# Adding the second direction's decay from PSUM on VectorE, with a third buffer for the decay rows

## The chip, the cores and the metric

The kernel runs on one core of one Trainium2 chip. The time is the device time of one execution in microseconds (us); of several runs the median is given. The engines are TensorE (PE in the profile, its weight loads PEld), VectorE (DVE), ScalarE (ACT), GpSimd (POOL) and SyncE (SP), which here only issues DMAs. The program is built by a tile framework: the code says what is computed and how many buffers each kind of tile has, and a scheduler puts the instructions of each engine in an order. Each engine then works through its own list strictly in that order.

## The reference

One inference step of a two-layer diffusion backbone over T = 1280 tokens (256 context, 1024 latent). Layer 0 is latent attention beside a convolution module; layer 1 is a bidirectional state-space mixer (SSD). The change lies in layer 1's scan, which the reference computes once per direction, in chunks of 128 tokens:

```
a_cum  = cumsum(dt * a_neg)                      # per chunk and head
decay  = exp(where(causal, a_cum[l] - a_cum[s], -inf))
cb     = einsum('bclgn,bcsgn->bclsg', c, b)
y_diag = einsum('bclsg,bclsge,bcsgep->bclgep', cb, decay, x * dt)
states = einsum('bcsgn,bcsge,bcsgep->bcgepn', b, exp(a_end - a_cum), x * dt)
prev   = scan over chunks: s = s * exp(a_end) + states
y_off  = einsum('bclgn,bcgepn,bclge->bclgep', c, prev, exp(a_cum))
y      = y_forward + flip(y_backward) + d_skip * x
out    = rmsnorm(y * silu(z)) @ w_out
```

The two directions share `x`, `b` and `c`; only the decays and the states differ.

## The kernel before

The kernel runs in stages: projection, convolution and attention of layer 0, the output projection and norm, then layer 1. Large matmuls are done as three products of split operands (`mm3`, lines 119 to 121).

The scan is a loop over eight passes `u` (four of the 32 heads each) and ten chunks `c` (lines 1219 to 1276). While pass `u` is scanned, the input projection and convolution of pass `u + 1` (`in_blocks`) and the gate blocks (`z_block`) are computed, and the backward states of pass `u + 1` are advanced, one chunk for each chunk scanned (`back_states`, through `bk`). Pass 7 has no next pass; its companions are the first parts of the output projection (`part_c`, tile `yh`, `yl`).

For a chunk, `scan_a` (line 1129) makes the 128x128 decay matrix of four heads for each direction: a matmul of the cumulated sums (`lt`, `mv`; line 1136) and one that adds the mask (line 1140) into a PSUM tile, and the exponential on ScalarE into an SBUF tile `et` (line 1141). GpSimd adds the two directions' tiles (line 1148), VectorE multiplies the sum by `cb` (line 1149). `scan_b` (line 1152) then takes the product of the states with `c` (line 1161) and of the decay with `x` (line 1166) into two more PSUM tiles, and VectorE puts them together: line 1170 multiplies by the rows `eb`, line 1175 sums over directions, 1178 and 1179 finish `y`. The squares of `y` are written into `eb` by ScalarE (1181) and added up by GpSimd (1183, 1184); only then is that `eb` free. `advance` (line 1070) steps a state: VectorE weights `x` (`xw`, line 1075), a matmul (1078), GpSimd scales the old state (1083), VectorE adds the matmul's result (1085). The backward `advance` first loads its own operand `bx` (line 1073).

PSUM has eight tiles here: three "mm" for the projections, one "tm" for transposes and four "sd", which the scan's tiles share in turn: two decay tiles, in even passes one for `cb`, the two of `scan_b`, and one for each `advance`.

Each chunk's inputs come by DMA: `xa` (three buffers), `eb` (two buffers, three DMAs, lines 1123 and 1126), `bx` (two), the mask rows `mv` and `lt` (two pairs of buffers, lines 1113 and 1114), `bt` and the prepared states `pl`. `y` goes out at line 1265, backward states at 1100. All stand in the one queue of SyncE, in order: a DMA whose buffer isn't free holds up all behind it.

The scheduler orders each engine's list by a simulated timeline, so an edit in one place moves instructions elsewhere as well.

Of the kernel before, what the change touches and what calls it, by code (L numbers as in the profile page):

```python
# [10 lines left out]
F32 = mybir.dt.float32  # L11
# [3 lines left out]
AF = mybir.ActivationFunctionType  # L15
# [41 lines left out]
def _body(nc, tc, d, es, dbg, stop):  # L57
    V, S, G, PE = nc.vector, nc.scalar, nc.gpsimd, nc.tensor
    dma = nc.sync.dma_start

    def pool(name, bufs=1, space=None, side=None, stack=es):
        kw = {}
        if space is not None:
            kw["space"] = space
        if side is not None:
            kw["side"] = side
        if space is None:
            kw["reuse_waits"] = "tile"
        return stack.enter_context(tc.tile_pool(name=name, bufs=bufs, **kw))
# [17 lines left out]
    def psum(tag="x"):  # L87
        tag = tag if tag in ptags else "sd"
        p, n = ptags[tag]
        return p.tile([128, 512], F32, name="ps" + tag, tag=tag, bufs=n)  # L90
# [91 lines left out]
    def bcast_cols(r, j0, jn, ps):  # L182
        for j in range(jn):
            PE.matmul(ps[:, j * 128:(j + 1) * 128], r[:, j0 + j:j0 + j + 1].to_broadcast([128, 128]), ident,
                      start=True, stop=True)
        return ps
# [246 lines left out]
    for c0, n in CHUNKS:  # L433
        ps = psum()
# [86 lines left out]
    for c0, n in CHUNKS:  # L521
        ps = bcast_cols(rq, c0 // 128, n // 128, ps=psum("pt"))
# [366 lines left out]
    def dtile(name, dt=F32, tag=None):  # L889
        return dq.tile([128, HT], dt, name=name, tag=tag or name)  # L890
# [40 lines left out]
    p = dtile("p")  # L931
# [43 lines left out]
    for half in range(2):  # L975
        hs = slice(half * 64, half * 64 + 64)
        for c0 in range(0, 5):
            c = half * 5 + c0
            ps = psum("sd")
# [77 lines left out]
    sp = pool("ssd", bufs=2, side="right", stack=esC)  # L1057
# [50 lines left out]
    xas, ebs, cbs, bts = {}, {}, {}, {}  # L1108
# [7 lines left out]
    def load_x(u, c):  # L1116
        xa = xas[c] = sp.tile([128, OXD], F32, name="xa", tag="xa", bufs=3)
        dma(xa, cmb[u, c, :, 0:OXD])
        if u % 2 == 0:
            bts[c] = sp.tile([128, 128], F32, name="bt", tag="bt")  # L1120
            dma(bts[c], cmb[u, c, :, OBT:OBT + 128])
        eb = ebs[c] = sp.tile([128, 2, 3, 128], F32, name="eb", tag="eb")
        dma(eb[:, :, 2], cmb[u, c, :, OXD:OXD + 256].rearrange("p (j t) -> p j t", j=2))
        for pr_ in range(2):
            ev = eyd[c, 4 * u:4 * u + 4].rearrange("(j p) d t -> p j (d t)", p=2)[pr_]
            dma(eb[pr_ * 64:pr_ * 64 + 64, :, 0:2].rearrange("p j d t -> p j (d t)"),
                ev.unsqueeze(0).to_broadcast([64, 2, 256]))

    def scan_a(u, c):
        xa = xas[c]  # L1130
        ct = xa[:, OCT:OCT + 128]
        mv, lt = mvs[c % NMV], lts[c % NMV]
        pss = [psum("sd") for _ in range(2)]
        es_ = [sp.tile([128, 4, 128], F32, name="et", tag="et", bufs=4) for _ in range(2)]
        for dr, ps in enumerate(pss):
            PE.matmul(ps, lt[:, dr], mv, start=True, stop=False)  # L1136
        for dr, ps in enumerate(pss):
            et = es_[dr].rearrange("p h t -> p (h t)")
            p3, mk = ps.rearrange("p (h t) -> p h t", h=4), maskb[:, dr:dr + 1].to_broadcast([128, 4, 128])
            PE.matmul(p3, identb, mk, start=False, stop=True)  # L1140
            S.activation(et, ps, AF.Exp)  # L1141
        if u % 2 == 0:
            pc_ = psum("sd")
            PE.matmul(pc_[:, :128], bts[c], ct, start=True, stop=True)
            cbs[c] = sp.tile([128, 128], F32, name="cb", tag="cb", bufs=NCH)
            S.copy(cbs[c], pc_[:, :128])
        mt = es_[0]
        G.tensor_add(mt, es_[0], es_[1])  # L1148
        V.tensor_mul(mt, mt, cbs[c].unsqueeze(1).to_broadcast([128, 4, 128]))
        return xa, mt  # L1150

# [67 lines left out]
    for u in range(8):  # L1219
# [9 lines left out]
        elif u:  # L1229
            z_block(2 * u)  # L1230
            z_block(2 * u + 1)
        load_x(u, 0)
        load_x(u, 1)
        if u == 7:
            esK.close()
# [4 lines left out]
            for k in range(14):  # L1240
                prep_y(0, k, None, yp[k < 6], "yhl")
        nxt = scan_a(u, 0)
        sf = None
        for c in range(NCH):
            cur, nxt = nxt, (scan_a(u, c + 1) if c + 1 < NCH else None)
            if c + 2 < NCH:
                load_m(u, c + 2)
# [11 lines left out]
            if c + 2 < NCH:  # L1259
                load_x(u, c + 2)  # L1260
# [281 lines left out]
```

## Time and profile before

| | us |
|---|---|
| median of 3 runs (2082.36 to 2091.7) | 2087.28 |
| the profiled execution, whole | 2085.1 |
| its span, first to last instruction | 2083.3 |
| TensorE busy | 1999.5 |
| VectorE busy | 1391.4 |
| ScalarE busy | 876.8 |
| GpSimd busy | 707.3 |

Busy time says how much of the span an engine had an instruction at work; TensorE's matmuls overlap, and the end of one is modelled, so that 96% doesn't mean full speed. The granted clock is the mean over the stretch of TensorE's two levels, 1.2 and 2.4 GHz, with 2.4 as 1. An idle time is put down to what ended it. The scan runs from about 1094 to 1880 us: the first chunk's mask matmul starts at 1094.4 us, and the last product of a decay tile at 1876.3 us.

### The profile page before, as it was taken

To read this page: it belongs to the slowest core of one execution; us is meant where nothing else is said; L and a number is where in the kernel's file an instruction comes from. 1 tells how busy PE (TensorE), PEld (TensorE's weight loads), DVE (VectorE), ACT (ScalarE), POOL (GpSimd) and SP (SyncE) were. 2 spreads that over 40 slices of the span, in tenths; PEclk is the share of its full clock that TensorE was granted. 3 is DMA by queue.
4 is the path that set the end of the run, shared out by engine and by line. 5 is a ranking of instruction groups with operands and counts; after the bars stand their busy time and mean duration, and the time that the engine had idled before them with its cause. 6 is when DMAs were issued, how large, how long until landed. Compare 5 with 4: busy or idle time off the path is not lost. (4 is left out here: it accounts for less than half of the span.)

```text
span 2083.3 us, 32430 instructions
## 1 busy us (share of the span) xinstructions
PE 1999.5 (96%) x11830; PEld 1629.6 (78%) x11830; DVE 1391.4 (67%) x2177; ACT 876.8 (42%) x1683; POOL 707.3 (34%) x567
## 2 busy tenths in 40 slices
PE   6999999999999999989999999999999999789997
PEld 4777888777777768868887878887788877579997
DVE  5797897666565763357658586758587666773743
ACT  5411311666565663234644343443344333334531
POOL 1211122213131212543125465545464444552101
PEclk9999999999999999999999999999999999999998
DMA  8424123220222225322567767765776577655442
GB/s 331 170 107 149 53 93 122 75 68 29 62 61 60 67 84 206 124 88 79 163 197 227 223 182 216 227 193 178 214 218 192 178 228 221 210 155 203 133 163 71
DMA packets 273341, 313.57 MB, mean 151 GB/s; under 512 B 21184, under 2 KB 221920, under 8 KB 273184
## 3 DMA queue, kind: packets, MB, share of 16 engines
q1 hardware_dynamic: 273184, 311.51, 47.6%
q8 instruction: 94, 1.54, 0.3%
q14 instruction: 63, 0.52, 0.1%
HBM read 223.38 MB, written 88.05 MB: 149 GB/s over the span
## 5 line engine op out<-in xcount | busy, mean ns | idle before, releaser
L119 PE MATMUL psmm<-hl,wh 128*128 128x512 f32 (+1 forms) x1152 | 424.1, 368 | 4.6 <-ACT wh L114 3.4
L121 PE MATMUL psmm<-hl,wl 128*128 128x512 f32 (+1 forms) x1152 | 422.2, 367 | 4.2 <-POOL wl L115 4.2
L120 PE MATMUL psmm<-hl,wh 128*128 128x512 f32 (+1 forms) x1152 | 423.7, 368 | 0.0
L115 POOL TENSOR_TENSOR wl<-ws,wh 128x1024 fp32r<-128x1024 f32 x89 | 224.5, 2524 | 464.2 <-ACT wh L114 462.1
L121 PEld LDWEIGHTS psmm<-hl,wl 128*128 128x128 f32 x1152 | 218.7, 190 | 36.9 <-POOL wl L115 6.2
L119 PEld LDWEIGHTS psmm<-hl,wh 128*128 128x128 f32 x1152 | 219.0, 190 | 35.9 <-ACT wh L114 4.3
L120 PEld LDWEIGHTS psmm<-hl,wh 128*128 128x128 f32 x1152 | 219.0, 190 | 30.1 <-issue 1.2
L383 DVE SCALAR_TENSOR_TENSOR cacc<-cvin,acw,cacc 128x1295 f32<-128x1295 f32 x120 | 206.9, 1741 | 4.6 <-ACT cacc L378 3.1
L114 ACT CAST wh<-ws 128x1024 fp32r<-128x1024 f32 x109 | 113.5, 1042 | 206.4 <-PE psmm L120 149.2
L848 DVE SCALAR_TENSOR_TENSOR cy<-raw,prm,cy 128x1282 f32<-128x1282 f32 x96 | 162.9, 1697 | 23.6 <-ACT cy L845 15.7
L120 PE MATMUL psmm<-hlo,wh 128*128 128x512 f32 (+3 forms) x480 | 171.4, 358 | 0.0
L119 PE MATMUL psmm<-hh,wh 128*128 128x512 f32 (+3 forms) x480 | 167.7, 359 | 1.7 <-ACT hh L259 1.7
L121 PE MATMUL psmm<-hh,wl 128*128 128x512 f32 (+3 forms) x480 | 169.2, 355 | 0.0
L617 DVE TENSOR_REDUCE mx<-pss 128x1 f32<-128x512 f32 (+1 forms) x208 | 137.3, 668 | 35.3 <-PE pss L121 34.3
L119 PE MATMUL psmm<-yh,wh 128*128 128x256 f32 (+1 forms) x476 | 148.2, 315 | 3.3 <-ACT yh L1205 2.8
L120 PE MATMUL psmm<-yl,wh 128*128 128x256 f32 (+1 forms) x476 | 150.0, 317 | 0.5 <-DVE yl L1206 0.3
L1148 POOL TENSOR_TENSOR et<-et 128x512 f32<-128x512 f32 x80 | 125.1, 1564 | 72.1 <-ACT et L1141 69.7
L121 PE MATMUL psmm<-yh,wl 128*128 128x256 f32 (+1 forms) x476 | 147.8, 314 | 1.4 <-POOL wl L115 1.4
L1083 POOL TENSOR_TENSOR st<-st,dec_bc 128x256 f32<-128x256 f32 x104 | 82.9, 803 | 168.6 <-DVE st L1085 113.4
L626 ACT ACTIVATE prob<-pss,nm 128x512 f32<-128x512 f32 x192 | 130.2, 693 | 16.1 <-DVE nm L621 14.2
L646 PE MATMUL pspt<-ident,prob 128*128 128x128 f32 x800 | 121.7, 278 | 4.7 <-ACT prob L626 3.8
L652 ACT COPY ptile<-pspt 128x512 f32<-128x512 f32 (+1 forms) x144 | 81.2, 568 | 105.3 <-PE pspt L646 104.3
(336 smaller groups left out, 4151.1 us busy)
## 6 DMA issues: line engine op xcount, KB each, us to landing
xa<-cmb SPq DMA_DIRECT2D x80, 384.0 KB
wm<-in_wmod_dram SPq DMA_DIRECT2D x48, 512.0 KB
ws<-in_wc_dram SPq DMA_DIRECT2D x40, 512.0 KB
eb<-eyd SPq DMA_DIRECT2D x160, 128.0 KB
ws<-in_wco_dram SPq DMA_DIRECT2D x32, 512.0 KB
cmb<-xt SPq DMA_DIRECT2D x24, 640.0 KB
bx<-cmb SPq DMA_DIRECT2D x72, 192.0 KB
eb<-cmb SPq DMA_DIRECT2D x80, 128.0 KB
```

Source lines behind the costliest of these rows:

```text
L114: S.copy(wh, ws)
L115: (eng or G).tensor_sub(wl, ws, f32(wh))
L119: PE.matmul(ps, lh, rh, start=start, stop=False)
L120: PE.matmul(ps, lh, rl, start=False, stop=False)
L121: PE.matmul(ps, ll, rh, start=False, stop=stop_)
L383: V.scalar_tensor_tensor(cacc[i], cv[:, k:k + CO], acw[:, 31 * i + k:31 * i + k + 1], cacc[i], ALU.mult, ALU.add)
L617: V.tensor_reduce(mx[:, x:x + 1], ps[:, :n], axis=AX.X, op=ALU.max, negate=len(segs) == 1)
L626: S.activation(prob[:, c:c + n], ps[:, :n], AF.Exp, bias=nm, accum_out=sums[:, x:x + 1])
L646: PE.transpose(ps[:, x * 128:(x + 1) * 128], prob[:, (g + x) * 128:(g + x + 1) * 128], ident)
L848: V.scalar_tensor_tensor(y, raw[:, k:k + RO], ccw[:, 5 * blk + k:5 * blk + k + 1], y, ALU.mult, ALU.add)
L1083: G.tensor_mul(n.rearrange("p (h e) -> p h e", e=64), s.rearrange("p (h e) -> p h e", e=64), dec_ap(u, dr, c))
L1148: G.tensor_add(mt, es_[0], es_[1])
```

## The change

Three edits in two functions. The second direction's exponential is written back into its own PSUM tile and not into an `et` tile. VectorE adds it from there to the first direction's tile, in place of GpSimd's addition of two SBUF tiles. So there is one `et` tile a chunk, and of these three buffers, where there were four buffers for two a chunk. The rows `eb` get three buffers and not two.

```diff
-        eb = ebs[c] = sp.tile([128, 2, 3, 128], F32, name="eb", tag="eb")
+        eb = ebs[c] = sp.tile([128, 2, 3, 128], F32, name="eb", tag="eb", bufs=3)
...
         pss = [psum("sd") for _ in range(2)]
-        es_ = [sp.tile([128, 4, 128], F32, name="et", tag="et", bufs=4) for _ in range(2)]
+        mt = sp.tile([128, 4, 128], F32, name="et", tag="et", bufs=3)
         for dr, ps in enumerate(pss):
             PE.matmul(ps, lt[:, dr], mv, start=True, stop=False)
         for dr, ps in enumerate(pss):
-            et = es_[dr].rearrange("p h t -> p (h t)")
             p3, mk = ps.rearrange("p (h t) -> p h t", h=4), maskb[:, dr:dr + 1].to_broadcast([128, 4, 128])
             PE.matmul(p3, identb, mk, start=False, stop=True)
-            S.activation(et, ps, AF.Exp)
+            S.activation(ps if dr else mt.rearrange("p h t -> p (h t)"), ps, AF.Exp)
...
-        mt = es_[0]
-        G.tensor_add(mt, es_[0], es_[1])
+        V.tensor_add(mt, mt, pss[1].rearrange("p (h t) -> p h t", h=4))
         V.tensor_mul(mt, mt, cbs[c].unsqueeze(1).to_broadcast([128, 4, 128]))
```

The new addition is line 1146 of the changed kernel and the multiplication line 1147; lines behind it are two lower than before.

Since the scheduler orders anew, the lists of all engines differ from the first chunk on. Three places matter. The first is SyncE's queue near the end of pass 6, before the change: `yz_16809` is the store of chunk 5, and `bx_16908` is the operand of the backward state step that goes with chunk 6.

```order
L1118 DMA xa_16834<-cmb_8593 128x768
L1106 DMA pl_16873<-pvd_9085 128x256
L1123 DMA eb_16772<-cmb_8593 128x2x128
L1126 DMA eb_16772<-eyd_8597 64x2x256 x2
L1100 DMA pvd_9085<-st_16848 128x256
L1121 DMA bt_16902<-cmb_8593 128x128
L1265 DMA yzd_8594<-yz_16809 128x2x128
L1118 DMA xa_16900<-cmb_8593 128x768
L1073 DMA bx_16908<-cmb_8593 128x384
```

The `bx` of chunk 6 stands behind the store of chunk 5; those of chunks 7 and 8 stand further on, between the stores of chunks 6 and 7. The same queue after the change: `yz_16742` is the store of chunk 5, and `bx_16905` the operand that goes with chunk 7.

```order
L1121 DMA bt_16834<-cmb_8593 128x128
L1114 DMA lt1_9078<-ltd_8596 8x128
L1123 DMA eb_16771<-cmb_8593 128x2x128
L1126 DMA eb_16771<-eyd_8597 64x2x256 x2
L1100 DMA pvd_9085<-st_16781 128x256
L1073 DMA bx_16905<-cmb_8593 128x384
L1113 DMA mv1_9077<-mvd_8595 2x512
L1263 DMA yzd_8594<-yz_16742 128x2x128
```

Now the `bx` of chunk 7 stands in front of the store of chunk 5; that of chunk 6 stands in front of the store of chunk 4, and that of chunk 8 in front of the store of chunk 6.

The second place is TensorE's list there. Before, at chunk 6, with the semaphores that each waits for:

```order
L1166 MATMUL pssd_16881<-et_16789,xa_16768 64x128 x3
L1078 MATMUL pssd_16895<-xw_16893,xa_16768 128x256 [waits Activation_49]
L1078 MATMUL pssd_16912<-xw_16910,bx_16908 128x256 [waits DMAHW0_49,DVE_49,Activation_49]
L1136 MATMUL pssd_16919<-mv0_9073,lt0_9074 128x512 [waits DMAHW2_49,DMAHW3_49,DMAHW1_49,PE_49]
L1136 MATMUL pssd_16920<-mv0_9073,lt0_9074 128x512 [waits DMAHW5_49]
```

The forward step's matmul waits for ScalarE, which frees its PSUM tile. After the change, at chunk 7:

```order
L1164 MATMUL pssd_16878<-et_16788,xa_16767 64x128 x3
L1078 MATMUL pssd_16892<-xw_16890,xa_16767 128x256 [waits DVE_49]
L1078 MATMUL pssd_16909<-xw_16907,bx_16905 128x256 [waits DMAHW5_49,DVE_49]
L1136 MATMUL pssd_16915<-mv1_9077,lt1_9078 128x512 [waits DMAHW6_49,DMAHW1_49,DVE_49]
L1139 LDWEIGHTS identb_8588
```

The order of the matmuls is the same; the forward step's matmul and the mask matmul behind it now wait for VectorE.

The third place is VectorE's list in the same stretch. Before:

```order
L1170 TENSOR_TENSOR eb_16772<-pssd_16876,eb_16772 128x2x2x128
L1149 TENSOR_TENSOR et_16855<-et_16855,cb_16865 128x512
L1175 TENSOR_REDUCE yz_16875<-eb_16772 128x256
L1085 TENSOR_TENSOR st_16897<-st_16897,pssd_16895 128x256
L1178 TENSOR_TENSOR yz_16875<-pssd_16881,yz_16875 128x256
```

After, the addition stands apart from the multiplication of the same tile:

```order
L1146 TENSOR_TENSOR et_16853<-et_16853,pssd_16852 128x512
L1177 TENSOR_TENSOR yz_16807<-yz_16807,xa_16702 128x256
L1168 TENSOR_TENSOR eb_16771<-pssd_16873,eb_16771 128x2x2x128
L1147 TENSOR_TENSOR et_16853<-et_16853,cb_16862 128x512
L1085 TENSOR_TENSOR st_16894<-st_16894,pssd_16892 128x256
L1075 TENSOR_TENSOR xw_16948<-xa_16832,dte_8592 128x256
```

The addition L1146 is a new instruction in this list, and the multiplication by `eb` (L1168), which waits for a load, can stand between it and the multiplication of the tile or in front of it.

## Rows read from the trace of the kernel before

**Rows 1.** The page: busy time by engine, and the granted clock in 40 slices.
```profile
PE 1999.5 (96%) x11830; PEld 1629.6 (78%) x11830; DVE 1391.4 (67%) x2177; ACT 876.8 (42%) x1683; POOL 707.3 (34%) x567
...
PEclk9999999999999999999999999999999999999998
```

**Rows 2.** Windows: span, busy PE, PEld, DVE, ACT, POOL (instructions), clock, DMA share, GB/s.
```profile
1094.00:1755.00 661.00, 652.25 (x3826) 531.88 (x3827) 468.77 (x670) 257.52 (x455) 335.89 (x314) 1.00 0.70 207
1755.00:1795.00 40.00, 27.07 (x138) 20.38 (x138) 23.48 (x46) 9.85 (x22) 19.00 (x25) 0.79 0.65 203
1795.00:1880.00 85.00, 75.49 (x511) 63.76 (x510) 65.92 (x98) 31.13 (x55) 50.99 (x47) 0.98 0.57 175
```

**Rows 3.** TensorE's waits, 1094 to 1755 us: us, times, longest.
```profile
PE pssd L1136 <- DVE eb L1170: 4.1, 4, 1.6
PE pssd L1136 <- DVE st L1085: 3.0, 4, 0.9
PE pssd L1078 <- DVE xw L1075: 1.2, 1, 1.2
```

**Rows 4.** TensorE's waits, 1755 to 1795 us.
```profile
PE pssd L1078 <- DVE xw L1075: 8.5, 2, 4.4
```

**Rows 5.** Timeline, end of pass 6: start, us, engine, line, operation [idle before].
```profile
1769.35 0.31 SPq L1114 DMA_DIRECT2D lt<-ltd  x1
...
1776.13 0.46 SPq L1073 DMA_DIRECT2D bx<-cmb  x1
...
1778.49 0.41 DVE L1085 TENSOR_TENSOR st<-st,pssd 128x256 f32<-128x256 f32 x1
...
1780.18 0.42 DVE L1075 TENSOR_TENSOR xw<-bx,dte 128x256 f32<-128x256 f32 x1 [0.30 <-DMA bx<-cmb]
...
1780.71 1.19 PE L1078 MATMUL pssd<-xw,bx 128*128 128x256 f32 x2 [4.41 <-DVE xw L1075]
...
1780.74 0.26 SPq L1113 DMA_DIRECT2D mv<-mvd  x1
...
1783.85 1.06 PE L1161 MATMUL pssd<-xa,st 128*128 128x128 f32 x4
...
1786.61 0.90 SPq L1073 DMA_DIRECT2D bx<-cmb  x2
...
1790.68 0.67 PE L1078 MATMUL pssd<-xw,bx 128*128 128x256 f32 x2 [4.09 <-DVE xw L1075]
```

**Rows 6.** Groups by line, whole span: busy us, mean ns | idle before.
```profile
L1148 POOL TENSOR_TENSOR et<-et 128x512 f32<-128x512 f32 x80 | 125.1, 1564 | 72.1 <-ACT et L1141 69.7 <-DMA xa<-cmb 1.2 <-DMA eb<-eyd 0.8
...
L1149 DVE TENSOR_TENSOR et<-et,cb 128x512 f32<-128x512 f32 x80 | 67.1, 839 | 51.3 <-POOL et L1148 47.3 <-ACT cb L1146 4.0
...
L1141 ACT ACTIVATE et<-pssd 128x512 f32<-128x512 f32 x160 | 91.7, 592 | 68.4 <-PE pssd L1140 68.0
...
L1170 DVE TENSOR_TENSOR eb<-pssd,eb 128x512 f32<-128x512 f32 x64 | 43.8, 685 | 47.2 <-PE pssd L1161 22.9 <-DMA eb<-eyd 21.0 <-DMA cmb<-cy 1.9
```

**Rows 7.** Instructions of lines 1149 and 1178: ns least/median/most.
```profile
L1149 DVE TENSOR_TENSOR et<-et,cb x80: 672/692/2883, 1102.4 to 1866.9; 128x512 f32<-128x512 f32 x80
...
L1178 DVE TENSOR_TENSOR yz<-pssd,yz x70: 407/416/426, 1107.2 to 1801.2; 128x256 f32<-128x256 f32 x70
```

**Rows 8.** The DMA queue's own waits, 1090 to 1880 us.
```profile
SPq L1123 <- POOL ysq L1184: 31.4, 29, 2.6
```

**Rows 9.** The chain that ended last, pass 7: start, us, what.
```profile
1834.13 1.45 POOL et L1148
...
1844.82 7.25 DMA eb<-eyd
```

**Rows 10.** VectorE's waits, 1795 to 1880 us.
```profile
DVE eb L1170 <- DMA eb<-eyd: 9.9, 5, 4.4
DVE et L1149 <- POOL et L1148: 6.0, 3, 2.6
```

**Rows 11.** VectorE's waits, 1090 to 1800 us.
```profile
DVE eb L1170 <- DMA eb<-eyd: 11.9, 3, 5.3
```

## The prediction

> **What bounds the kernel now.** I read the page's busy shares first, then the stages, then TensorE's waits stage by stage, and last the DMA queue. TensorE is busy 96% of the span and its granted clock is full nearly everywhere [rows 1], so no time can come from doing less elsewhere. The change takes nothing from TensorE, since the same matmuls run; it can only win or lose TensorE's idle time and low clock in the scan. The reader is to see three stages of very different kind [rows 2]. In passes 0 to 6 up to 1755 us TensorE idles 661.00 - 652.25 = 8.75 us. In the end of pass 6 (1755 to 1795 us), where no input-projection matmul is left to fill in, it idles 40.00 - 27.07 = 12.93 us, and the clock is 0.79, a mixture of its two levels, 2.4 and 1.2 GHz, after gaps. In pass 7 it idles 85.00 - 75.49 = 9.51 us at clock 0.98. All that can be won is thus 31 us of gaps, and what the clock costs: 27.07 us of work at 0.79 would take 21.4 us at full clock, 5.7 us less.
>
> What ends the gaps differs. Up to 1755 us the two largest waits are for a free PSUM tile of the shared tag "sd": 4.1 us until VectorE has read the products with the states (L1170) and 3.0 us until it has read the state update (L1085); 1.2 us are for an operand, `xw` [rows 3]. At the end of pass 6, two waits of 4.4 and 4.1 us make 8.5 of the 12.9 us, both before the backward state matmul L1078 [rows 4]. They are really waits for a DMA: `bx` is requested at 1776.13 us, VectorE can form `xw` at 1780.18 us and TensorE goes on at 1780.71; the second is requested at 1786.61 and TensorE goes on at 1790.68 us [rows 5]. The load takes some 4 us and was asked for late.
>
> **The change part by part.** *Removed:* 80 Pool additions of mean 1564 ns, 125.1 us of Pool [rows 6]. VectorE was idle 47.3 us in front of its multiply L1149 for them.
>
> *Added:* 80 VectorE additions of 128x512 with one PSUM operand. The row of that shape is L1170, 685 ns [rows 6], so 80 x 0.685 = 54.8 us. They take the place of 47.3 us in which VectorE stood still; 7.5 us are left. Against these stands that VectorE's operations on two SBUF operands lengthen when Pool works beside them: L1149 has a median of 692 and a maximum of 2883 ns, while L1178 with a PSUM operand stays between 407 and 426 [rows 7]. L1149 alone loses 80 x (839 - 692) ns = 11.8 us to that, and its own Pool addition is a part of what runs beside it. So VectorE is about as late in its queue as before; I count 0, between -11.8 and +7.5, none of it directly on TensorE.
>
> *The exponential:* the second one writes back into its PSUM tile. The trace has no ScalarE write into PSUM. The nearest row is the present one, 592 ns [rows 6]; I let it be up to that much shorter or longer, 80 x 0.592 = 47 us of ScalarE either way, which is busy 42% [rows 1], and count 0. The cover is that share, and if ScalarE were late the masks' PSUM tiles would free later, which belongs to the next point.
>
> *Held longer:* the second decay tile used to be free after its exponential, and now is free after VectorE's addition. Four "sd" tiles serve six or seven requests a chunk. In the order, the forward L1078 behind the mask pair now waits for VectorE where it waited for ScalarE. Behind it in TensorE's queue stand the backward L1078 and the next mask pair. In front of the addition in VectorE's queue stand operations such as L1168 that wait for DMAs. Bounds: nothing, if fillers cover it, as they cover most of the four VectorE releases a chunk now (L1085 twice, L1170, L1178); and 54.8 us, if each of the 80 additions stood whole on TensorE's path. Nearest is [rows 3]: 4.1 + 3.0 = 7.1 us for four releases a chunk, so a fifth costs about 1.8 us. I take +2.
>
> At this point the Trainium skill speaks against the change: "ScalarE: Activation LUTs", section "Step-by-step: what each stage is for", calls PSUM the quicker destination for an activation, but only useful where TensorE does not need most of PSUM. Here TensorE uses all eight banks (3 + 1 + 4 tiles), which the waits of [rows 3] show. By its first half the sum stays, since ScalarE is not late; by its caveat it is the slower rival below.
>
> *The third `eb` buffer:* `eb` is freed only when Pool has added the squares (L1184). The DMA queue stands in order, and at its `eb` requests it waited 31.4 us for Pool 29 times, with all requests behind it [rows 8]. With a third buffer that wait goes to the `eb` of a chunk earlier. What the order shows at the end of pass 6 is what I rest on: the `bx` of chunk 7 stood behind the `y` store of chunk 6 and now stands in front of that of chunk 5; the `bx` of chunk 6 stood behind the store of chunk 5 and now stands in front of that of chunk 4. With 4 us to land and these two chunks 10 us apart (1780.71 to 1790.68), they come in time. What is late next? The mask rows for the matmuls behind the gaps had been asked for long before (the last at 1769.35 and 1780.74 [rows 5]). Behind them stands the product that reads the state, 3.1 us after the late L1078 (1780.71 to 1783.85). Without the gap, which began at 1780.71 - 4.41 = 1776.30, it would come at 1779.4 or, at full clock, earlier. VectorE's state update began at 1778.49, and the new addition may stand in front of it, 0.685 us. So the state is about as late as TensorE, and I give back one addition for each gap: -8.5 + 1.4 = -7.1, with bounds 0 (the state or `xa` takes the whole place) and -8.5.
>
> *The clock:* 5.7 us hang on the gaps of that stage. Of its 12.93 us of gaps 7.1 go, 55%, so I take 55% of it, -3.1, between 0 and -5.7.
>
> *Pass 7:* Pool's `et` addition stands on the chain that ended last (1.45 us), before the squares that free `eb`, of which a load soon after takes 7.25 us [rows 9]. VectorE waits 9.9 us for `eb` loads in this pass and 6.0 us for Pool's `et` [rows 10]. But VectorE is busy 65.92 of 85 us [rows 2] and gets 10 x 0.685 = 6.9 us more. Bounds -9.5 (all idle time) and +6.9; I take -2.5, what two such additions on the chain less most of one addition's 0.685 us leave (2 x 1.45 - 0.4).
>
> *Third `et` buffer instead of two pairs:* nothing waits there; 0.
>
> The sum: +2.0 - 7.1 - 3.1 - 2.5 = -10.7 us. The profiled execution took 2085.1 us (span 2083.3 and 1.8 around it), which makes 2074.4; it lies 2.2 us under the median 2087.3, so I forecast 2076.6 as a median.
>
> **The rivals.** *Slot rival (slower).* VectorE's additions stand behind L1168 and `xw`, which wait for loads. While VectorE waits, the PSUM tile is held and TensorE stops at the next L1078 or mask pair; Pool's addition was never behind those waits. Price: VectorE's waits for `eb` are 11.9 us up to 1800 [rows 11] and 9.9 us in pass 7 [rows 10]; if TensorE shares them all and the gains fail, 2087.3 + 21.8 = 2109. It decides from the point where the added waits pass the 12.7 us of gains. For it: TensorE is in order and already waits for these tiles. Against: in most chunks input-projection matmuls stand between, and the third `eb` buffer shortens just those waits.
>
> *Hidden rival (no change).* The early `bx` only uncovers the next late thing at the end of pass 6: the `xa` rows, the state chain through VectorE and Pool, or the queue's own issue work. Then the gaps stay, the Pool work removed was never on TensorE's path, and the time is 2087 +- 5. For it: Pool is busy 34% and TensorE waits almost nowhere for it directly. Against: only 1.2 us of `xw` waits in the 661 us before, so where `bx` is asked for early it costs almost nothing.
>
> *Larger gain.* Both stages close: 8.5 + 5.7 of pass 6's end and 9.5 of pass 7, 23.7 us, gives 2064. Against it stands VectorE's load in pass 7.
>
> **How the numbers follow.** Forecast 0.50 (its own range 2066 to 2087), hidden rival 0.25, slot rival 0.17, larger gain 0.08. A measurement of this kernel tells about 0.5% from no change, 10.4 us, so faster means under 2076.8. The forecast lies at that bound: 0.30 of its 0.50 is below it, with the larger gain 0.38. Slower are nearly all of the slot rival and little else, 0.17. The rest, 0.45, is within. The range leaves out a tenth on each side: the larger gain beyond 2061, and the slot rival beyond 2099.
>
> **What would show it.** Right: at the end of pass 6 no wait of L1078 for `xw` over 2 us, idle time there under 7 us and a clock above 0.85; Pool's busy time near 582 us; VectorE's near 1391 + 55 less some 10 to 25; the waits of mask and state matmuls for VectorE up by 2 us or so before the end of pass 6. Wrong: L1078 waiting for the new addition (L1146) by more than 10 us in sum (slot rival); or the same 12 us of gaps at the end of pass 6, ended by `xa`, `st` or mask rows (hidden rival).

## The result, and the profile after

The changed kernel takes 2061.8 us in the median of four runs (2056.3 to 2065.3), the kernel before 2085.5 beside it: ratio 0.989, 95% interval 0.9874 to 0.9907, or 23.7 us less. The forecast was 2076.6, 10.7 us less than the 2087.3 from which it started. The direction came as said; the size is more than twice the forecast. The profiled execution took 2060.95 us.

The page of the changed kernel, busy time by engine and granted clock [rows 1]:

```profile
PE 1993.4 (97%) x11830; PEld 1626.0 (79%) x11830; DVE 1415.9 (69%) x2257; ACT 882.3 (43%) x1683; POOL 578.7 (28%) x487
...
PEclk8999999999999999999999999999999999999998
```

GpSimd has lost the 125 us of its additions and VectorE has 24.5 us more. The added operation costs 54.4 us (below), so all else on VectorE takes 29.9 us less of its busy time. Some 5.5 us of this are overlap of neighbouring instructions, which busy time counts once: summed by instruction, VectorE takes 1492.4 us before and 1522.4 us after, so all else became 24.4 us shorter. The forecast has no such number.

Stages that end at the same events in both kernels are compared best: the last input-projection matmul, the first mask matmul of pass 7, the last product of a decay tile, the end. These are the windows of the kernel before, cut at these events (columns as in [rows 2]):

```profile
1094.00:1748.20 654.20, 645.45 (x3777) 525.78 (x3778) 465.19 (x665) 254.65 (x450) 332.22 (x312) 1.00 0.70 206
1748.20:1798.50 50.30, 37.20 (x214) 28.92 (x212) 30.41 (x56) 12.72 (x28) 22.67 (x27) 0.83 0.69 220
1798.50:1876.60 78.10, 68.76 (x464) 57.92 (x463) 60.64 (x89) 31.04 (x55) 48.59 (x46) 0.98 0.58 177
1876.60:2083.30 206.70, 193.89 (x1333) 193.21 (x1333) 107.20 (x200) 76.01 (x127) 23.92 (x18) 0.97 0.42 142
```

And of the changed kernel:

```profile
1094.00:1739.90 645.90, 645.90 (x3804) 528.12 (x3803) 484.85 (x732) 259.91 (x453) 225.58 (x248) 1.00 0.71 211
1739.90:1780.90 41.00, 34.95 (x229) 28.10 (x228) 34.36 (x62) 14.07 (x28) 18.02 (x22) 0.96 0.73 218
1780.90:1848.50 67.60, 60.38 (x407) 49.41 (x405) 56.62 (x98) 28.26 (x51) 31.10 (x35) 0.95 0.68 208
1848.50:2059.10 210.60, 197.62 (x1356) 197.00 (x1354) 111.67 (x200) 77.19 (x127) 24.03 (x19) 0.97 0.42 139
```

Stage by stage that is -8.3, -9.3, -10.5 and +3.9 us, together -24.2. Companion matmuls move between the last two stages (464 and 1333 before, 407 and 1356 after), so these are read together: -6.6. In the first stage TensorE's idle time falls from 8.75 us to nothing: the forecast had +2.0 there. The three waits for VectorE that [rows 3] lists in this stage, 4.1 + 3.0 + 1.2 us, are as much as it gained.

TensorE's waits of the changed kernel, 1094 to 1870 us (us in total, times, longest) [rows 3, 4]:

```profile
PE pssd L1143 <- issue: 3.4, 1, 3.4
PE psmm L119 <- ACT yh L1203: 3.1, 1, 3.1
PE pstm L1164 <- DVE ylast L1176: 1.2, 3, 0.5
PE psmm L119 <- DMA lt<-ltd: 1.2, 1, 1.2
PE pstm L1164 <- DVE et L1147: 1.0, 1, 1.0
```

No mask matmul is among these waits with VectorE as its cause, no L1078 for `xw`, and none for the new addition (L1146). VectorE's groups in the same stretch, of which the second fence shows one of the kernel before [rows 6]:

```profile
L1147 DVE TENSOR_TENSOR et<-et,cb 128x512 f32<-128x512 f32 x80 | 59.7, 747 | 5.8 <-ACT cb L1145 3.8 <-DVE et L1146 0.5
...
L1146 DVE TENSOR_TENSOR et<-et,pssd 128x512 f32<-128x512 f32 x80 | 54.4, 680 | 31.0 <-ACT pssd L1140 31.0
...
L1177 DVE TENSOR_TENSOR yz<-yz,xa 128x256 f32<-128x256 f32 x70 | 38.3, 548 | 0.9
```

```profile
L1179 DVE TENSOR_TENSOR yz<-yz,xa 128x256 f32<-128x256 f32 x70 | 46.4, 663 | 0.9
```

The 47.3 us that the multiply by `cb` stood waiting for GpSimd became 31.0 us in which the addition waits for ScalarE, and operations that the change doesn't touch got shorter. The waits for loads of `eb` [rows 8, 10, 11], now (VectorE's, then those of SP's queue, same stretch):

```profile
DVE eb L1168 <- DMA eb<-eyd: 1.7, 2, 1.2
```

```profile
SPq L1123 <- POOL ysq L1182: 21.8, 29, 2.1
```

ScalarE's two exponentials differ by 8 ns:

```profile
L1140 ACT ACTIVATE et<-pssd 128x512 f32<-128x512 f32 x80 | 47.7, 596 | 85.8 <-PE pssd L1139 85.6
L1140 ACT ACTIVATE pssd<-pssd 128x512 f32<-128x512 f32 x80 | 47.1, 588 | 18.5 <-PE pssd L1139 16.5 <-DVE yl L1204 1.4
```

### The profile page after: what moved, and what is told of

Same layout as the page of the kernel before. It is cut to its first block, busy times and chain, and to the rows that moved or that the text cites. A ratio compares the mean times of both kernels' runs of the same rounds, so it can differ in the third digit from the quotient of the medians.

```text
span 2059.1 us, 32474 instructions
## 1 busy us (share of the span) xinstructions
PE 1993.4 (97%) x11830; PEld 1626.0 (79%) x11830; DVE 1415.9 (69%) x2257; ACT 882.3 (43%) x1683; POOL 578.7 (28%) x487
## 4 chain that ended last, share of the span: by engine, by line
PE 90%; DVE 3%; DMA 2%; ACT 1%; issue 1%; SPq 1%; POOL 0%; DVEq 0%; ACTq 0%; POOLq 0%
PE psmm L119 18%; PE psmm L120 18%; PE psmm L121 18%; PE pspo L666 5%; PE pspt L646 4%; PE pssd L1078 3%; PE pss L119 3%; PE pssd L1159 3%; PE pss L121 3%; PE pss L120 3%; PE pssd L1164 2%; PE pssd L1136 2%; PE pssd L1139 2%; PE psx L229 1%; PE pstm L1036 1%
## 5 line engine op out<-in xcount | busy, mean ns | idle before, releaser
L383 DVE SCALAR_TENSOR_TENSOR cacc<-cvin,acw,cacc 128x1295 f32<-128x1295 f32 x120 | 206.9, 1740 | 4.6 <-ACT cacc L378 3.1
L848 DVE SCALAR_TENSOR_TENSOR cy<-raw,prm,cy 128x1282 f32<-128x1282 f32 x96 | 157.2, 1637 | 24.6 <-ACT cy L845 17.0
L646 PEld LDWEIGHTS pspt<-ident,prob 128*128 128x128 f32 x800 | 92.1, 141 | 40.4 <-ACT prob L626 10.2
```

The costliest lines, as they stand in the source:

```text
L383: V.scalar_tensor_tensor(cacc[i], cv[:, k:k + CO], acw[:, 31 * i + k:31 * i + k + 1], cacc[i], ALU.mult, ALU.add)
L646: PE.transpose(ps[:, x * 128:(x + 1) * 128], prob[:, (g + x) * 128:(g + x + 1) * 128], ident)
L848: V.scalar_tensor_tensor(y, raw[:, k:k + RO], ccw[:, 5 * blk + k:5 * blk + k + 1], y, ALU.mult, ALU.add)
```

## The experiments

What had to be told apart was where 23.7 us came from: **A**, VectorE no longer stands in its order behind GpSimd's result; **B**, the third `eb` buffer; **D**, GpSimd's work itself, which lengthens VectorE's operations; **C**, the new order that the scheduler makes of any edit. This is TensorE's idle time (window less busy) in the four stages, from each profile, beside the medians and ratios; the fences of before and after above are its first two rows. A profiled execution isn't always near its median: that of e1d is 5.6 us under it, that of h2 5.0 us over it.

| kernel | median us | ratio (95%) | idle: to last input proj. | end of pass 6 | pass 7 | rest |
|---|---|---|---|---|---|---|
| before | 2085.5 | | 8.8 | 13.1 | 9.3 | 12.8 |
| changed | 2061.8 | 0.989 (0.9874-0.9907) | 0.0 | 6.0 | 7.2 | 13.0 |
| e2 | 2066.5 | 0.9916 (0.9903-0.9929) | 0.1 | 6.8 | 10.2 | 12.5 |
| e1d | 2081.1 | 0.9981 (0.9969-0.9993) | 5.2 | 14.7 | 6.3 | 12.8 |
| e3 | 2077.1 | 0.9966 (0.9954-0.9979) | 4.1 | 12.8 | 7.8 | 12.9 |
| h1 | 2075.9 | 0.9960 (0.9945-0.9976) | 4.6 | 8.1 | 12.1 | 12.9 |
| h2 | 2077.0 | 0.9969 (0.9958-0.9979) | 4.1 | 10.4 | 8.0 | 14.6 |
| g1 | 2068.2 | 0.9918 (0.9903-0.9933) | 0.0 | 13.6 | 5.2 | 12.8 |
| j1 | 2082.8 | 0.9989 (0.9979-1.0000) | 7.9 | 10.3 | 5.7 | 14.1 |
| l1 | 2077.3 | 0.9967 (0.9956-0.9979) | 4.1 | 14.6 | 7.0 | 12.3 |
| l2 | 2078.6 | 0.9974 (0.9964-0.9983) | 2.6 | 13.2 | 8.6 | 12.9 |
| i1 | 2089.4 | 1.0022 (1.0012-1.0031) | 7.1 | 12.6 | 10.9 | 12.1 |
| g2 | 2084.0 | 0.9995 (0.9986-1.0005) | 8.0 | 15.7 | 7.2 | 12.9 |

**The parts of the change.** e2, the change without its third `eb` buffer:

```diff
-        eb = ebs[c] = sp.tile([128, 2, 3, 128], F32, name="eb", tag="eb", bufs=3)
+        eb = ebs[c] = sp.tile([128, 2, 3, 128], F32, name="eb", tag="eb")
```

> The change without its third eb buffer: the addition moves from Pool to VectorE and reads PSUM, eb keeps two buffers. Theory A (VectorE no longer stands 47.3 us in its order behind Pool's addition, so it reads the shared PSUM tiles earlier, and TensorE's waits for those tiles go): the 9.2 us gained up to the last input-projection matmul stay, the waits of TensorE for VectorE there stay under 2 us (7.6 + 3.0 before), and only the end of pass 6 falls back; time 2068 to 2074. Theory B (the third buffer gives it: VectorE's waits for eb loads, 11.9 + 9.9 us before, hold the PSUM tiles): the gain is lost, TensorE's waits for eb and st are back near 10 us, time 2082 to 2092, since VectorE has 54 us more to do.

Measured 2066.5: 18.0 of the 23.7 us stand without the buffer, and the first stage keeps its gain (644.8 us), as A said (the 9.2 us named there come from a cut 0.9 us too early; at the event itself it is 8.3). But the time is under A's range, since the end of pass 6 did not fall back (43.1 us, clock 0.96), which no theory had.

e1d, the kernel before with the third `eb` buffer, paid with one `et` buffer:

```diff
-        eb = ebs[c] = sp.tile([128, 2, 3, 128], F32, name="eb", tag="eb")
+        eb = ebs[c] = sp.tile([128, 2, 3, 128], F32, name="eb", tag="eb", bufs=3)
...
-        es_ = [sp.tile([128, 4, 128], F32, name="et", tag="et", bufs=4) for _ in range(2)]
+        es_ = [sp.tile([128, 4, 128], F32, name="et", tag="et", bufs=3) for _ in range(2)]
```

> The kernel before with a third eb buffer alone, paid with one of its four et buffers; Pool keeps the addition. Theory A: TensorE's waits for eb and st before the end of pass 6 stay near 10 us, and only the end of pass 6 improves (its two waits for xw, 8.5 us, and the clock); time 2072 to 2080. Theory B: those waits fall under 3 us, and the time is 2062 to 2070. If both parts are needed together, it is 2083 to 2089. The lost et buffer may cost some us of ScalarE's waits for the matmuls that read et, which would show there.

Measured 2081.1, 3.3 us less than before. TensorE's waits at the end of pass 6 (1740 to 1791.9 us) in e1d:

```profile
PE pssd L1078 <- DVE xw L1075: 10.2, 2, 5.6
PE psmm L119 <- ACT yh L1205: 3.0, 1, 3.0
```

The two waits for `xw` are still there. So the buffer is not what brings `bx` early.

e3, the addition on VectorE with both exponentials still in SBUF:

```diff
-        G.tensor_add(mt, es_[0], es_[1])
+        V.tensor_add(mt, es_[0], es_[1])
```

> The kernel before with the addition on VectorE and nothing else: both exponentials still go to SBUF, so no PSUM tile is held longer, and the addition has two SBUF operands. Theory A: what counts is that Pool leaves VectorE's path; the waits of TensorE for VectorE go as in the change, time 2068 to 2076, with the addition at 650 to 850 ns instead of 680. If the PSUM operand itself matters (the Pool beside it lengthens operations on two SBUF operands): addition near 850 ns or above, time 2078 to 2088. Theory B: 2082 to 2092, as without the buffer nothing is won.

Measured 2077.1, 7.4 us less than before, and 844 ns for the addition. The waits for VectorE that [rows 3] shows are nearly gone in e3, 1094 to 1740 us:

```profile
PE pstm L1036 <- ACT xt L1037: 1.4, 1, 1.4
PE pssd L1078 <- ACT et L1141: 1.1, 1, 1.1
PE pssd L1161 <- DVE st L1085: 0.8, 1, 0.8
```

e3 takes away both VectorE's wait in its order (A) and GpSimd's additions (D), and has a third of the whole gain. e7, the changed kernel with two `et` buffers:

```diff
-        mt = sp.tile([128, 4, 128], F32, name="et", tag="et", bufs=3)
+        mt = sp.tile([128, 4, 128], F32, name="et", tag="et", bufs=2)
```

> The changed kernel with two et buffers instead of three. If nothing waits for et, as I counted, the time is that of the changed kernel, 2060 to 2064, and no ScalarE wait for an et reader appears. If the third buffer is part of the gain (ScalarE's exponential runs ahead only with it), ScalarE waits for the last reader of et, the masks' PSUM tiles free later, and the time is 2066 or more.

Measured 2058.9 (ratio 0.9878, 0.9863 to 0.9892): the third `et` buffer is worth nothing. Against e2 on the same chip, 2066.5, the third `eb` buffer is worth 7.6 us here; against the changed kernel itself 4.6.

**GpSimd's and VectorE's work by itself.** e4 and e8, e2 with an idle addition a chunk on GpSimd or on VectorE:

```diff
+    pdum = sp.tile([128, 512], F32, name="pdum", bufs=1)
+    G.memset(pdum, 0.0)
...
+        G.tensor_add(pdum, pdum, pdum)     # e8: V.tensor_add
```

> The version with two eb buffers and the addition on VectorE (18 us faster than before), to which one idle addition of 128x512 in place on Pool is added in each chunk; nobody reads its result, so Pool has its old work back but nobody waits for it. Theory A (VectorE's in-order wait for Pool's result was the cost): Pool's busy time is back near 707, the time stays within 5 us of 2066. Theory D (Pool's work beside VectorE lengthened its SBUF operations and delayed the squares that free eb): VectorE's operations on two SBUF operands lengthen again and 7 or more of the 18 us are lost, 2074 or more.

> The same version, to which one idle addition of 128x512 in place on VectorE is added in each chunk (80 x some 0.7 us = 55 us of VectorE, nobody reads it). If VectorE's added work costs nothing as the sum had it (the term 0 for the 54.8 us), the time stays within 4 us of 2066. If VectorE's work is paid in the end of pass 6 and in pass 7, where few fillers stand, it is 2072 to 2082, and the loss stands in these stages; each chunk's addition whole on the path would be 2121.

Measured 2097.3 and 2097.6, slower than the kernel before. The additions depend on nothing, and the scheduler put all 80 in one heap (instructions of that line in e4, then in e8: ns least/median/most, first and last start):

```profile
L1148 POOL TENSOR_TENSOR pdum<-pdum x80: 1032/1162/2294, 1013.8 to 1184.9; 128x512 f32<-128x512 f32 x80
```

```profile
L1148 DVE TENSOR_TENSOR pdum<-pdum x80: 673/688/2897, 1019.3 to 1167.5; 128x512 f32<-128x512 f32 x80
```

The loss stands at the heap: from 1040 us to the start of the third pass e2 takes 240 us and e4 268, and from there to the last input projection 459 both. They say nothing on a steady load. h1 and h2 tie the addition to the chunk's finished tile:

```diff
+    pdum = sp.tile([128, 4, 128], F32, name="pdum", bufs=1)
...
         V.tensor_mul(mt, mt, cbs[c].unsqueeze(1).to_broadcast([128, 4, 128]))
+        G.tensor_add(pdum, mt, mt)     # h2: V.tensor_add
```

> The version with two eb buffers and the addition on VectorE (18 us faster than before), to which Pool makes one idle addition of 128x512 in each chunk, reading the chunk's finished decay tile, so that it comes once a chunk and not in a heap; its result is not used. Theory A (VectorE's wait in order for Pool's result was the cost): 2064 to 2072, TensorE's waits for VectorE before the end of pass 6 stay under 2 us. Theory D (Pool's work itself, by lengthening VectorE's operations and delaying the squares, was the cost): 2076 to 2085.

> The same with the idle addition on VectorE, also tied to the chunk's finished decay tile (80 x 0.7 to 0.8 us = 56 to 64 us more VectorE work). If VectorE's added work is hidden, as the sum had it for the change's own addition: 2064 to 2072. If it is paid where fillers are few (end of pass 6 and pass 7, 20 additions): up to 14 us more, 2075 to 2081.

Measured 2075.9 and 2077.0: 9.5 and 10.5 us more than e2 (8.7 and 9.8 when each is held against the kernel before beside it). That is at the edge of D's range for h1, and against the sum for h2. h1 is the cleanest comparison of the study: by the traces only 435 of TensorE's 11,830 matmuls stand elsewhere in its order than in that of e2, where every other kernel has 740 or more. Busy times in e2, then in h1, with the instructions of `xw` from `xa`, `yz` and the addition from PSUM (ns least/median/most; or busy us, mean):

```profile
PE 1994.8 (97%) x11830; PEld 1625.6 (79%) x11830; DVE 1410.7 (68%) x2257; ACT 880.5 (43%) x1683; POOL 581.7 (28%) x487
```

```profile
L1075 DVE TENSOR_TENSOR xw<-xa,dte x71: 406/417/727, 1107.5 to 1846.8; 128x256 f32<-128x256 f32 x71
```

```profile
L1146 DVE TENSOR_TENSOR et<-et,pssd 128x512 f32<-128x512 f32 x80 | 54.4, 680 | 35.1 <-ACT pssd L1140 35.0
...
L1177 DVE TENSOR_TENSOR yz<-yz,xa 128x256 f32<-128x256 f32 x70 | 37.8, 540 | 0.9
```

```profile
PE 1997.4 (96%) x11830; PEld 1626.0 (78%) x11830; DVE 1446.8 (70%) x2257; ACT 879.9 (42%) x1683; POOL 671.5 (32%) x567
```

```profile
L1075 DVE TENSOR_TENSOR xw<-xa,dte x72: 407/423/1830, 1097.0 to 1847.4; 128x256 f32<-128x256 f32 x72
```

```profile
L1148 DVE TENSOR_TENSOR et<-et,pssd 128x512 f32<-128x512 f32 x80 | 54.3, 679 | 23.1 <-ACT pssd L1142 22.9
...
L1180 DVE TENSOR_TENSOR yz<-yz,xa 128x256 f32<-128x256 f32 x70 | 46.4, 663 | 0.9
...
L1150 POOL TENSOR_TENSOR pdum<-et 128x512 f32<-128x512 f32 x80 | 88.1, 1101 | 150.6 <-DVE et L1149 136.4 <-DMA eb<-eyd 6.1 <-DVE st L1085 5.1
```

VectorE does the same 2257 instructions, and 1446.8 - 1410.7 = 36.1 us more of time. GpSimd's additions took 88.1 us (1101 ns each). The median of `xw` hardly moves (417 and 423 ns); the longest ones and the mean do (438 and 619 ns). What grew are operations on two SBUF operands. Summed by instruction, all of VectorE takes 37.4 us more; instructions that combine two tensors in SBUF account for 36.1 of it, and the 964 that read PSUM for -0.4.

Up to the last input-projection matmul e2 takes 644.8 us and h1 652.4, so 7.6 us of the loss stand in this stage, and the waits of TensorE listed there in h1 all end with VectorE (1094 to 1746.4 us):

```profile
PE pssd L1162 <- DVE yz L1179: 1.8, 2, 1.4
PE pssd L1167 <- DVE st L1085: 1.3, 1, 1.3
PE pssd L1078 <- DVE xw L1075: 1.2, 1, 1.2
PE pssd L1078 <- DVE et L1148: 0.2, 1, 0.2
```

The idle addition isn't wholly off the path. The chunk's `et` tile is free only when GpSimd has read it, and ScalarE waits for that four times in the scan, once (2.4 us) in this stage:

```profile
ACT et L1142 <- POOL pdum L1150: 7.5, 4, 2.4
```

So h1 gives the price of GpSimd's load as a whole. How much of it comes through VectorE's longer operations, through GpSimd's other work coming later or through the held tile isn't separated. h2 is less clean: its order differs from e2's in 2545 matmuls, and 10.8 us of its loss stand at the end of pass 6 (53.9 against 43.1 us), 5.1 before.

**The end of pass 6.** i1, the kernel before asking for `bx` one step ahead:

```diff
-            s = advance(s, u, c, 1, tag="pv" if c - 1 in KEEP else "st")
+            o, nb = nb, load_b(u, c - 1) if c > 3 else None
+            s = advance(s, u, c, 1, bx=o, tag="pv" if c - 1 in KEEP else "st")
```

> The kernel before, in which each backward step asks for the bx of the next step ahead of its own work, so one chunk earlier; buffers and everything else as before. The step of the prediction on the end of pass 6 said that the two late bx requests cost 8.5 us of waits and with the clock 10 us. If that is right: no wait of TensorE for xw over 2 us there, the stage 50 to some 40 us, time 2072 to 2078. If another thing is late next (states, mask rows): the waits change their name and the time stays 2081 to 2088.

Measured 2089.4, no gain, and 4.3 us more than the kernel before beside it. TensorE's waits at the end of pass 6 in i1 (1745 to 1795.3 us):

```profile
PE psmm L119 <- ACT yh L1214: 4.5, 1, 4.5
PE pssd L1153 <- DMA bt<-cmb: 4.3, 2, 3.2
PE pssd L1145 <- ACT et L1150: 1.4, 2, 0.7
```

The waits for `xw` went, and `yh` and `bt` are late in their place: the stage still takes 50.3 us. This is the hidden rival of the prediction, for this step. g2, the kernel before with a third `bx` buffer (and three `et`):

```diff
-            bx = sp.tile([128, 384], F32, name="bx", tag="bx")
+            bx = sp.tile([128, 384], F32, name="bx", tag="bx", bufs=3)
```

> The kernel before with a third bx buffer, paid with one of four et buffers; nothing else. It asks whether the 8.5 us of TensorE's waits for xw at the end of pass 6, and the clock there, hang on the late request of bx. If so, those waits go, the stage falls from 50.2 to some 42 us and the time is 2072 to 2078. If the request is late because of what stands in front of it in SP's list and not for want of a buffer, the waits stay and the time is 2081 to 2088.

Measured 2084.0, the same as before, with 7.4 us of `xw` in one wait: a missing buffer isn't why the request is late, which leaves its place in SP's list. i2, e7 with the edit of i1:

> The changed kernel with two et buffers (the fastest so far, 2059) and the same earlier request of bx. It waits for xw nowhere at the end of pass 6, so by the theory that bx was the cause there it gains nothing: 2056 to 2062. If the new order that any such edit brings matters more than what it does: more than 4 us either way.

Measured 2061.6 (ratio 0.9887, 0.9874 to 0.9900): nothing, as expected.

**The tile held longer.** g1, e3 with a small read that holds the second decay tile; j1, the same behind GpSimd's addition in the kernel before; l1, the small read without the hold; l2, the hold one operation longer:

```diff
         V.tensor_add(mt, es_[0], es_[1])
+        V.tensor_add(pdum, mt[:, 0, :1], pss[1][:, :1])   # g1; j1 behind G.tensor_add; l2 behind the multiply
+        V.tensor_add(pdum, mt[:, 0, :1], mt[:, 1, :1])    # l1 instead
```

> The addition on VectorE with both exponentials in SBUF (7 us faster than before), to which VectorE reads one column of the second decay tile in PSUM behind each addition, so that this tile is held as long as in the change. If the 10.6 us between that version and the one that adds from PSUM come from the new order of instructions that the longer hold brings, this is near 2066. If they come from the PSUM operand (addition 680 against 844 ns, 13 us of VectorE, and ScalarE's write), it is 2077 to 2085, by up to 80 x 0.1 us more for the small reads. If holding costs as the sum had it, +2, it is 2079 to 2087.

> The kernel before (Pool adds, both exponentials in SBUF), to which VectorE reads one column of the second decay tile in PSUM behind Pool's addition, so that the tile is held till then; 80 reads of some 0.14 us = 11 us more of VectorE. If the longer hold gains by the order that it brings, whoever adds: 2072 to 2079. If holding a PSUM tile behind an engine that waits is what the prediction feared: 2086 or more, TensorE's waits for VectorE before the end of pass 6 above 12 us. If the order's gain needs the addition on VectorE: 2080 to 2087.

> The addition on VectorE with both exponentials in SBUF (2077 us), to which VectorE makes the same small operation of one column in each chunk as in the kernel that holds the tile (2068), but reads SBUF alone, so that no PSUM tile is held. If the hold is what gained 9 us: 2074 to 2082, idle time of TensorE up to the last input-projection matmul 3 us or more. If the gain was the luck of one order: 2064 to 2072 is as likely.

> The same with the small read of the PSUM tile behind VectorE's multiply and not behind its addition: held by one operation of some 0.8 us more. If the hold gains: 2063 to 2072, TensorE idle under 1 us up to the last input-projection matmul. If it was the luck of one order: 2074 or more is as likely.

Measured 2068.2, 2082.8, 2077.3 and 2078.6. g1 alone would have made the hold a gain of 9 us. j1 shows 2.7 us of gain at most, and the feared waits are there, 1094 to 1740 us:

```profile
PE pssd L1138 <- DVE eb L1173: 5.1, 2, 2.6
PE pssd L1078 <- DVE pdum L1151: 2.1, 4, 0.8
```

l2 holds longer still and has lost the gain of g1, most of it in pass 7 (80.5 against 73.2 us), although its idle time in the first stage is low too (2.6 us). The orders of g1 and e3 differ in 2949 of the 11,830 matmuls. So kernels that differ by one small read a chunk lie 9 us apart either way, and the hold as such isn't shown to gain.

**Versions meant to be better,** all on top of e7: k1 has both VectorE operations on a PSUM operand, k3 a fourth `eb` buffer, e6 a third `bx` buffer.

```diff
-        V.tensor_add(mt, mt, pss[1].rearrange("p (h t) -> p h t", h=4))    # k1
-        V.tensor_mul(mt, mt, cbs[c].unsqueeze(1).to_broadcast([128, 4, 128]))
+        p1 = pss[1].rearrange("p (h t) -> p h t", h=4)
+        V.tensor_add(p1, mt, p1)
+        V.tensor_mul(mt, p1, cbs[c].unsqueeze(1).to_broadcast([128, 4, 128]))
...
-    STB = {"st": 6, "pv": 6, "pl": 3}    # k3, with eb bufs=4
+    STB = {"st": 5, "pv": 6, "pl": 2}
...
-            bx = sp.tile([128, 384], F32, name="bx", tag="bx")    # e6
+            bx = sp.tile([128, 384], F32, name="bx", tag="bx", bufs=3)
```

> The changed kernel with two et buffers (2059), in which VectorE's addition writes back into the PSUM tile and its multiply by cb reads it from there: both operations have a PSUM operand and the tile is held by one more operation. If operations on two SBUF operands are what Pool's work lengthens: the multiply falls from 754 to 690 ns or less, VectorE has 5 us less to do, time 2054 to 2060. If the longer hold costs, or the new order does: 2062 to 2070.

> The same version with a fourth eb buffer, paid with one st and one pl buffer. Only 1.7 us of VectorE's waits for eb loads are left, so nothing is to be won: 2056 to 2062; if the smaller st and pl pools cost, 2063 or more.

> The same version with a third bx buffer. SP's queue stands 34 us at bx requests until L1078 frees a buffer, with all requests behind it. If that holds up loads that TensorE waits for, it is 2050 to 2056; since TensorE waits for no load before the end of pass 6, I expect no change there, 2056 to 2062.

Measured 2065.4 (0.9911, 0.9896 to 0.9925), 2068.5 (0.9925, 0.9911 to 0.9940) and 2061.5 (0.9889, 0.9874 to 0.9904). In k1 the multiply fell to 684 ns as said and VectorE to 1394.8 us, and yet the time rose: two waits for `xw`, 9.1 us, are back at the end of pass 6. k3 lies where its expectation put a cost of the smaller `st` and `pl` pools. No version is shown to beat the changed kernel; e7, with less memory, is at least as fast.

## Why the prediction was wrong

The step that failed is the part of the sum up to 1755 us: *Added* at 0 and *Held longer* at +2.0, where the first stage measured -8.3 us. The other parts came nearer: -9.3 against -10.2 us at the end of pass 6, and -6.6 against -2.5 behind it.

- *Added.* The duration was right (680 ns, forecast 685). The relief of VectorE was mis-sized: the forecast counted up to 11.8 us, on the multiply alone. The multiply got 7.4 of them (67.1 to 59.7 us), but all of VectorE's other work together became 24.4 us shorter, and VectorE's busy time, 1415.9 us, is under the 1421 to 1436 that was to show the forecast right. "None of it directly on TensorE" was wrong as well: [rows 3] has 8.3 us of waits for VectorE in this stage, and with an earlier VectorE they went. h1 supports this by experiment: 88 us of GpSimd work put back beside VectorE lengthen VectorE by 36 us and cost 9.5 us of time, 7.6 of them in this stage. I read the waits and gave an earlier VectorE no share in them.
- *Held longer.* After the change L1078 never waits for the addition, and the waits from which I took +1.8 are gone. The mechanism exists: j1 shows it with 2.1 us where VectorE waits for GpSimd. But e3 shows that moving the addition off GpSimd already clears TensorE's waits for VectorE, with 4.1 us of idle time left in the stage.
- *The exponential* and *the third `et` buffer*, 0 each, were right (588 and 596 ns; e7).
- *The third `eb` buffer and the clock*, -7.1 and -3.1 at the end of pass 6: the stage measured -9.3, the waits for `xw` went, and the clock rose to 0.96, all as said, but not for the reason said, so that the number came close is luck. e1d has the buffer and keeps the waits; e2 lacks it and has the gain; i1 has `bx` early and no gain. The buffer's own gain is 4.6 us on top of the rest, 3.3 alone. From e2 to the changed kernel the stages move by +1.1, -2.1 and, from pass 7 on, -5.5 us, so most of it stands from pass 7 on, where VectorE's waits for `eb` loads in pass 7 are 7.7 us in e2 and 1.7 in the changed kernel. Over the scan these waits fell from 21.8 us [rows 10, 11] to 1.7, those of SP's queue for a free buffer from 31.4 [rows 8] to 21.8.
- *Pass 7*, -2.5: with the rest of the program -6.6. *Larger gain*, the rival nearest in time (2064), put all of it into these two stages and none into the first.

The Trainium skill's "ScalarE: Activation LUTs" ("Step-by-step: what each stage is for") spoke against the change where TensorE needs most of PSUM. In the trace after it, the waits for a free PSUM tile of [rows 3] are gone; and the quicker destination gives 8 ns of 596.

A path of steps that the runs allow: from before to h1 -9 us (the addition off GpSimd's path, while GpSimd is as loaded as it was to some 5%), from h1 to e2 -9.5 (GpSimd's load gone), from e2 to the change -4.6 (the buffer). In the first stage alone, where the forecast failed, these steps are -1.8, -7.6 and +1.1 us in the profiles. The middle step has nearly one order and is the surest. The first step isn't separated from the new order that comes with it: 6.3 of its 7.2 us in the profiles stand at the end of pass 6.

**Open.** e3 and e2 differ by 10.6 us, in the PSUM operand (13 us less of VectorE) and in the hold; h2's 10.5 us for 64.5 us of additions would make some 2 of these, an estimate, since h2's price holds its own change of order. The rest goes with the scheduler's order. Of TensorE's 11,830 matmuls, 435 to 1434 stand elsewhere than in e2 in the changed kernel, e4, e6, e7, e8, h1, i2 and k3, and all of these have a short end of pass 6 (41 to 44 us, as e2); 2114 to 3111 do in the other eleven kernels, and there it takes 50 to 58. The two go together in all the kernels compared, but that isn't yet a cause: the same instructions in another order weren't tried, as the scheduler sets it.

## What to carry to other kernels

When work leaves one of two engines that share operands in SBUF, count the relief on every operation of the other, and not only on the line that you edit. Mean less median, summed over all lines of VectorE, shows that there is something to win (116 us before), but isn't the forecast: 24.4 us came. Where the waits of the busiest engine end with that other engine, let the relief have a share in these waits, up to their sum. Where a scheduler orders the program, an edit of next to no work can move it by as much as the edit that you study: compare lists, and prefer the experiment whose list stays the same.

## What the runs showed of the hardware

GpSimd's 88 us of additions made VectorE's operations on two SBUF operands 36 us longer (the `xw` ones at most 727 ns without and 1830 with), while the 80 additions with a PSUM operand stayed within 670 and 689 ns beside the same GpSimd work (h1). The Trainium skill's "GPSIMD Engine Reference" ("Key points") states that the two engines contend where VectorE has two SBUF inputs; the traces agree, and give the price: 0.41 us of VectorE for each us of GpSimd here. An exponential on ScalarE written back into PSUM took 588 ns, into SBUF 596.
